# Two tiles of the second layer's attention ahead of its last query projection, and that projection's sink inside the attention pipeline

## The chip, the cores and the metric

The kernel runs as one program on one core of a Trainium2 chip. Its time is the device time of that core in microseconds (us); the times shown are medians of several runs, and the profile is of one further execution. PE is TensorE's matmul, PEld its weight load, DVE VectorE, ACT ScalarE, POOL GpSimd, SP SyncE, which issues the loads.

## The reference

A flow-matching backbone of two layers (0 and 1) with model width 1024, on 512 latent tokens and 256 context tokens. In layer 1, the last, only the latent tokens go on. Its attention half, cut to what matters:

```python
z_lat = h_lat @ w_in[l]                       # queries, keys, values, u and g in one projection
qh_l = apply_rope(rmsnorm(q_heads(q_l), q_norm_g[l]), cos, sin) * q_scale      # 8 query heads
kh_l = apply_rope(rmsnorm(kv_heads(k_l), k_norm_g[l]), cos, sin)               # 2 key heads
k_all = jnp.concatenate([kh_c, kh_l], axis=2)                                  # 256 + 512 keys
attn_lat = gqa_blocks(qh_l, k_all, v_all)                                      # softmax per query
gm_lat = chunk_gmlp(u_l, g_l, w_spatial[l], b_spatial[l], gmlp_norm_g[l])      # spatial gating
x_lat = x_lat + ga1 * (jnp.concatenate([attn_lat, gm_lat], axis=-1) @ w_out[l])
x_lat = x_lat + ga2 * sqrelu_mlp(modulate(rmsnorm(x_lat, norm2_g[l]), sh2, sc2), w_ff1[l], w_ff2[l])
```

## The kernel before

**Numbers in two parts.** Every operand of a large matmul is a pair: a high part in the fp32r format, and a low part, the rest. `split` (L226, L227) makes the pair, the high part by a cast on ACT and the low part by a subtraction on DVE or POOL. A product is three matmuls, high x high, high x low, low x high. All of them are recorded at L222, in the helper `mm`; what they do is told by their buffers.

**Layer 1 up to the attention.** The projection makes keys and values, u and g tiles, and at last the queries. `TokProj.bank` computes 256 tokens x 256 query columns into one PSUM bank (48 matmuls, in two halves of 24) and calls a sink. Four such banks give the queries: two groups (g) of four heads, two token pairs (tp) each; a head group belongs to one key head. PSUM banks of the tag b exist twice (`b0`, `b1`); `pb()` takes them in turn, or the one that `which` names. Tag a exists twice (two banks each, for scores), tag t twice (for transposes and the spatial mix).

The sink of a query bank, `sink_q`, calls `qk`: ACT squares the bank (L721), DVE sums the squares (L723), multiplies by the rotary tables (L727 and twice L731, which reads the bank last), forms the mean (L740); POOL adds the two products (L732), takes the power -1/2 (L313) and multiplies (L742). The result t1 lies in an SBUF tile of the tag w. `turned` then puts off, by the planner's count `fl.vt`, two more steps: a stack of high and low part (a cast on ACT at L747, a subtraction on DVE at L748) and its turn (8 transposes on PE at L760 and two casts on ACT at L761 into Q, `B3` to `B6`). The program calls these postponed turns the query turns; the attention forces those that it needs.

In the last query sink two things come first: the rest of the spatial mixes (`mixes`), and `make_gm`, which makes the pairs A0 to A3 of the gating output (casts L808 on ACT, subtractions L810 on DVE).

**The attention pipeline.** `pipeline` runs 32 tiles of 128 queries of one head against 768 keys, in 36 steps s. In a step stand, in this order: `scores(s)` on PE (4 matmuls into a PSUM tile pa; DVE takes the maximum, L1162), `turned_weights(s-2)` (6 transposes on PE, L1191, into two tiles pt; ACT casts them, L1193, DVE makes the low parts, L1194), `values` for the pair of tiles four steps back (6 matmuls per step, into a bank b0), `expo(s)` on ACT (L1171; its output is again a tile of the tag w, of which there are three), and one piece of filler. The filler, `out_pieces`, is the first half of the output projection, which needs the gating output alone: 32 pieces of 3 matmuls, four to a result, in bank b1; DVE adds each result to X (L1001). Steps 11, 12, 21 and 22 have no piece, step 2 has two. `mixed_heads` closes a pair of heads on DVE (L1221, L1223), and POOL writes the pair back into Q (L1225, L1226).

**What sets the order.** Up to the query banks a scheduler places the instructions on each engine by its own estimates; the whole of `pipeline` stands in `tc.manual_schedule` for PE, DVE and ACT, so there the order is that of the program text. On each engine the instructions then run in the order shown, each waiting for its own inputs and buffers.

Of the kernel before, what the change touches and what calls it, by code (L numbers as in the profile page):

```python
# [171 lines left out]
def trunk(ctx: ExitStack, tc: tile.TileContext, xT, pk1, pk2, rope, wsT, w_mod, w_tok, w_u, w_out, w_ff1, w_ff2, outT):  # L172
# [529 lines left out]
    def layer(l, h, nxt, K, kv=None, kv0=0):  # L702
# [11 lines left out]
        def qk(ps4, tp, nh, which, pool=False):  # L714
# [9 lines left out]
            t1 = te().rearrange("p (t h d) -> p t h d", t=2, h=nh) if pool and nh == 4 else tw([128, 2, nh, 64])  # L724
# [77 lines left out]
        def make_gm():  # L802
            for f in mixes:
                f()
            for g in range(4):
                gm = unit(f"A{g}", [128, 2, T])
                src = U[g // 2][:, g % 2, 0:TQ]
                act.copy(gm[:, 0, 0:TQ], src)  # L808
                with behind(maxes[3] if l == 0 and len(maxes) > 3 else None):
                    vec.tensor_tensor(out=gm[:, 1, 0:TQ], in0=src, in1=gm[:, 0, 0:TQ].bitcast(F32), op=ALU.subtract)  # L810
                GM.append(gm)

        def sink_q(grp):
            def f(tp, ps, pool=False):
                if tp == 0:
                    for f_ in mixes if grp and l else ():
                        f_()
                    Q.extend(unit(f"B{3 + grp * 2 + i}", [128, 2, T]) for i in range(2))
                ps = [p.rearrange("p (h d) -> p h d", d=64) for p in ps] if isinstance(ps, list) else ps.rearrange("p t (h d) -> p t h d", d=64)
                if last and grp and tp == NP - 1:  # L820
                    for f_ in mixes:
                        f_()
                    make_gm()
                t1 = qk(ps, tp, 4, 0, pool)
                turned(t1, 4, 0, tp, [(Q[grp * 2 + i], [(2 * i, 0), (2 * i + 1, 0)]) for i in range(2)], late(tp) + 4000.0 if pool else None)
            return f
# [163 lines left out]
        with region('q%d' % l):  # L990
            for g in range(2) if l else ():
                qp = TokProj(l, 1 + g, h, NP, sink_q(g))
                for tp in range(NP):
                    qp.bank(tp)
# [133 lines left out]

        def out_pieces():
            if not GM:  # L1130
                make_gm()
            for m in range(8):
                if m % 2 == 0:
                    wb = take("out", l, 0, m // 2)
                dst = pb(which=1)
                for k, (whi, wlo, rhi, rlo) in enumerate(w4(wb, m, GM)):
                    for i, (a, b) in enumerate(((whi, rhi), (whi, rlo), (wlo, rhi))):
                        mm(dst, a, b[:, 0:TQ], k == 0 and i == 0, k == 3 and i == 2, TQ)
                    if k < 3:
                        yield  # L1140
                gate(2, m, 0, TQ, dst)
                if m % 2:
                    release()
                yield

        def pipeline():
# [4 lines left out]
            pieces = out_pieces()  # L1151
# [45 lines left out]
            def values(g, half):  # L1197
                j, blk, hh, _ = tiles[2 * g]
                st = pairs[g // 2]
                if half == 0:  # L1200
                    st["o"] = pb(which=0)
# [15 lines left out]
            def mixed_heads(g):  # L1217
# [4 lines left out]
                if hh == 1:  # L1222
                    vec.tensor_tensor(out=mix, in0=o[:, 256:512], in1=mix, op=ALU.mult)  # L1223
                    b = slice(blk * 256, blk * 256 + 256)
                    pool_e.tensor_copy(Q[j][:, 0, b], mix)  # L1225
                    pool_e.tensor_tensor(out=Q[j][:, 1, b], in0=mix, in1=Q[j][:, 0, b].bitcast(F32), op=ALU.subtract)  # L1226
                    done[0] += 1

            for s in range(nt + 4):
                if s < nt:  # L1230
# [3 lines left out]
                    scores(s)  # L1234
                if s % 4 == 0 and 0 < s <= nt:
# [7 lines left out]
                for _ in range(0 if s in (11, 12, 21, 22) else 2 if s in (2,) else 1):  # L1243
# [4 lines left out]
            for _ in pieces:  # L1248
                fl.tick()
# [44 lines left out]
        if last:  # L1294
            fl.fillers.pop(0)
            state["slow"] = True
            with tc.manual_schedule(engines={mybir.EngineType.PE, mybir.EngineType.DVE, mybir.EngineType.Activation}):
                pipeline()
# [242 lines left out]
```

## Time and profile before

| | us |
|---|---|
| median of 3 runs (1477.64 to 1478.91) | 1478.48 |
| the profiled execution | 1480.37 |
| its span | 1478.5 |
| mean granted TensorE clock | 0.997 |

The profiled execution is 1.9 us above the median, and 1.9 us of it lie outside the span. Layer 1's last query bank and its attention stand at 981 to 1098 us of the span. A row of a timeline gives the start, the duration, the engine, the line, the operation with output and input tiles, the count, and in brackets how long the engine was idle before and what ended that. Matmuls overlap, so what one costs is read from start to start, not from its duration. The granted clock is 1.00 at full speed.

### The profile page before, as it was taken

What the parts mean: (1) busy time and instruction counts of PE and PEld (TensorE: products, weight loads), DVE (VectorE), ACT (ScalarE), POOL (GpSimd) and SP (SyncE); (2) the same over time, 40 slices, a digit from 0 to 9 for tenths busy, and PEclk for the clock granted to TensorE, in tenths of its full rate; (3) what the DMA queues carried; (4) which work ended last, traced back from release to release, by engine and by line L of the source; (5) the groups of instructions that cost most, each with busy time, mean ns of one, the idle gap of its engine ahead of it and who ended that gap; (6) DMA issues with size and microseconds to landing.
All of it is one profiled execution on the core that took longest, in us unless ns stands there. A gap on an engine that the chain in (4) does not pass through costs nothing.

```text
span 1478.5 us, 21039 instructions
## 1 busy us (share of the span) xinstructions
PE 1440.8 (97%) x8178; PEld 1227.3 (83%) x8178; DVE 911.8 (62%) x1594; ACT 638.7 (43%) x1133; POOL 369.5 (25%) x312
## 2 busy tenths in 40 slices
PE   6999999999999999999999999989999999999998
PEld 2899787988888888888888889988889888888887
DVE  5857867778766564645555547767868554444443
ACT  3552546665545443343434234537755323332221
POOL 0333512222256451323324122272222000000000
PEclk9999999999999999999999999999999999999999
DMA  9322544101233333334234212210001333223331
GB/s 368 111 72 96 191 145 143 58 1 58 95 123 126 112 134 107 129 114 134 96 124 134 76 41 75 86 58 30 30 29 63 123 100 100 94 92 100 100 100 57
DMA packets 50083, 148.71 MB, mean 101 GB/s; under 512 B 5440, under 2 KB 6976, under 8 KB 49984
## 3 DMA queue, kind: packets, MB, share of 16 engines
q1 hardware_dynamic: 49408, 146.72, 29.7%
q8 instruction: 64, 1.05, 0.3%
q10 hardware_dynamic: 576, 0.66, 0.2%
q14 instruction: 35, 0.29, 0.1%
HBM read 145.26 MB, written 2.10 MB: 100 GB/s over the span
## 4 chain that ended last, share of the span: by engine, by line
PE 86%; DVE 6%; ACT 3%; POOL 2%; issue 1%; DMA 1%; SPq 0%; POOLq 0%; ACTq 0%; DVEq 0%
PE pa L222 54%; PE pb L222 23%; PE pb L369 2%; PE pt L222 2%; PE pt L1067 2%; PE pt L1191 1%; POOL m L313 1%; ACT hi L226 1%; PE pt L760 1%; DVE lo L227 1%; DMA A<-in_w_mod 1%; POOL lo L227 1%; DVE s L922 0%; DVE X L1001 0%; DVE A L810 0%
## 5 line engine op out<-in xcount | busy, mean ns | idle before, releaser
L222 PE MATMUL pa<-A,hi 128*128 128x512 f32 (+2 forms) x1440 | 429.9, 376 | 0.6 <-DVE s L731 0.3
L226 ACT CAST hi<-raw 128x1024 fp32r<-128x1024 f32 x168 | 176.0, 1048 | 326.1 <-PE pa L222 243.3
L222 PEld LDWEIGHTS pa<-A,hi 128*128 128x128 f32 x1440 | 262.7, 188 | 46.8 <-DVE s L731 0.6
L222 PE MATMUL pa<-A,lo 128*128 128x512 f32 (+2 forms) x832 | 283.9, 347 | 0.0
L227 DVE TENSOR_TENSOR lo<-raw,hi 128x1024 fp32r<-128x1024 f32 x152 | 204.6, 1346 | 121.8 <-ACT hi L226 117.4
L418 POOL TENSOR_TENSOR C<-C,s 128x512 f32<-128x512 f32 x112 | 175.5, 1581 | 294.6 <-ACT s L417 287.8
L222 PE MATMUL pa<-B,hi 128*128 128x512 f32 x750 | 239.0, 392 | 0.0
L222 PEld LDWEIGHTS pa<-A,lo 128*128 128x128 f32 x832 | 156.7, 188 | 21.3
L1001 DVE SCALAR_TENSOR_TENSOR X<-pa,modT,X 128x512 f32<-128x512 f32 x168 | 99.7, 614 | 104.5 <-PE pa L222 103.0
L222 PEld LDWEIGHTS pa<-B,hi 128*128 128x128 f32 x750 | 139.9, 188 | 27.1
L222 PE MATMUL pb<-B,hi 128*128 128x512 f32 (+1 forms) x600 | 157.3, 350 | 2.1 <-DVE X L1001 2.0
L222 PE MATMUL pa<-B,lo 128*128 128x512 f32 (+1 forms) x450 | 155.3, 354 | 0.0
L222 PEld LDWEIGHTS pb<-B,hi 128*128 128x128 f32 x600 | 104.5, 189 | 17.5 <-DVE X L1001 3.4
L222 PE MATMUL pb<-hi,A 128*128 128x256 f32 (+1 forms) x608 | 118.1, 291 | 0.6 <-DVE m L740 0.6
L1001 DVE SCALAR_TENSOR_TENSOR X<-pb,modT,X 128x512 f32<-128x512 f32 (+3 forms) x116 | 70.7, 619 | 77.5 <-PE pb L222 77.3
L222 PE MATMUL pb<-B,lo 128*128 128x512 f32 (+1 forms) x300 | 104.0, 347 | 0.0
L222 PEld LDWEIGHTS pb<-hi,A 128*128 128x128 f32 x608 | 97.0, 191 | 2.2 <-PE pb L222 0.8
L222 PEld LDWEIGHTS pa<-B,lo 128*128 128x128 f32 x450 | 84.6, 188 | 14.8
L417 ACT ACTIVATE s<-k,silu 128x512 f32<-128x512 f32 x112 | 78.1, 718 | 37.3 <-DMA k<-in_w_mod 29.3
L222 PE MATMUL pb<-lo,A 128*128 128x256 f32 (+1 forms) x304 | 87.7, 288 | 0.0
L222 PE MATMUL pb<-A,hi 128*128 128x384 f32 (+2 forms) x288 | 82.1, 367 | 4.4 <-DVE m L740 3.4
L222 PE MATMUL pa<-B,B 128*128 128x256 f32 (+1 forms) x288 | 67.6, 350 | 0.0
(226 smaller groups left out, 2198.5 us busy)
## 6 DMA issues: line engine op xcount, KB each, us to landing
raw<-in_w_ff SPq DMA_DIRECT2D x128, 512.0 KB, 3.5
k<-in_w_mod SPq DMA_DIRECT2D x96, 256.0 KB, 2.8
raw<-in_w_tok SPq DMA_DIRECT2D x16, 512.0 KB, 3.5
raw<-in_w_out SPq DMA_DIRECT2D x16, 512.0 KB, 3.5
lo<-in_w_mod SPq DMA_DIRECT2D x16, 512.0 KB, 4.6
hi<-in_w_mod SPq DMA_DIRECT2D x16, 512.0 KB, 4.2
A<-in_w_mod SPq DMA_DIRECT2D x8, 512.0 KB, 10.0
B<-in_w_mod SPq DMA_DIRECT2D x8, 512.0 KB, 9.4
```

Of the source, the lines that this page charges most:

```text
L222: pe.matmul(out, a, b, start=start, stop=stop)
L226: act.copy(hi, src)
L227: (eng or vec).tensor_tensor(out=lo, in0=src, in1=hi.bitcast(F32), op=ALU.subtract)
L313: pool_e.tensor_tensor(out=y, in0=v, in1=mhalf[:, 0:n], op=ALU.pow)
L369: pe.matmul(ps[q:q + 32, :], S32[:, k, :], ws_[k2 // 2][:, k2 % 2 * 512:(k2 % 2 + 1) * 512], start=k < ns, stop=k >= KT - ns)
L417: act.activation(p, w, AF.Copy, scale=s)
L418: pool_e.tensor_tensor(out=a, in0=a, in1=p, op=ALU.add)
L760: pe.transpose(p[:, o:o + 128], stk[:, t, hh, c0:c0 + 128].bitcast(F32), ident)
L1001: vec.scalar_tensor_tensor(out=xs, in0=src[:, s - off:e - off], scalar=modT[l][:, i * 8 + m, cond:cond + 1], in1=xs, op0=ALU.mult, op1=ALU ...
L1067: pe.transpose(tp_[:, (kt - k0) * 128:(kt - k0) * 128 + 128], p[:, kt * 128:kt * 128 + 128], ident)
L1191: pe.transpose(tp_[:, kt * 128:kt * 128 + 128], p[:, (k0 + kt) * 128:(k0 + kt) * 128 + 128], ident)
```

## The change

The four query banks move from their own place to the place where the pipeline is called. Before the last of them (g = 1, tp = 1) come the mixes, `make_gm` and steps 0 and 1 of the pipeline; that bank is then computed and held, and its sink is called inside step 2, behind `scores(2)`. Fillers take the b bank that the last query bank does not hold, the values take the other. `make_gm` in layer 1 leaves the low parts of A2 and A3 to POOL. The t1 of layer 1's queries lie in tiles of the tag e instead of w (three of each). Steps 0 and 1 have no filler any more, nor 16 and 17, while 11, 12, 21 and 22 have one. The very last pair of heads is split on ACT and DVE, where POOL did both parts.

```diff
-            t1 = te().rearrange(...) if pool and nh == 4 else tw([128, 2, nh, 64])
+            t1 = te().rearrange(...) if (pool or l) and nh == 4 else tw([128, 2, nh, 64])
...
-                    vec.tensor_tensor(out=gm[:, 1, 0:TQ], in0=src, in1=gm[:, 0, 0:TQ].bitcast(F32), op=ALU.subtract)
+                    (pool_e if l and g > 1 else vec).tensor_tensor(out=gm[:, 1, 0:TQ], in0=src, in1=gm[:, 0, 0:TQ].bitcast(F32), op=ALU.subtract)
...
-                if last and grp and tp == NP - 1:
-                    for f_ in mixes:
-                        f_()
-                    make_gm()
...
-        with region('q%d' % l):
-            for g in range(2) if l else ():
-                qp = TokProj(l, 1 + g, h, NP, sink_q(g))
-                for tp in range(NP):
-                    qp.bank(tp)
...
-                dst = pb(which=1)
+                dst = pb(which=banks_[0])
...
-                    st["o"] = pb(which=0)
+                    st["o"] = pb(which=banks_[0] ^ 1)
...
+                    if 2 * g + 2 == nt:
+                        split(Q[j][:, 0, b], Q[j][:, 1, b], mix)
+                    else:
...
-            for s in range(nt + 4):
+            def step(s, between=None):
...
                     scores(s)
+                if between:
+                    between()
...
-                for _ in range(0 if s in (11, 12, 21, 22) else 2 if s in (2,) else 1):
+                for _ in range(0 if s < 2 or s in (16, 17) else 2 if s == 2 else 1):
                     next(pieces, None)
...
+            step, nt, rest = pipeline()
+            for g in range(2):
+                qp = TokProj(l, 1 + g, h, NP, sink_q(g))
+                for tp in range(NP):
+                    if g == 0 or tp < NP - 1:
+                        qp.bank(tp)
+                        continue
+                    for f in mixes:
+                        f()
+                    make_gm()
+                    step(0)
+                    step(1)
+                    q3 = qp.bank(tp, hold=True)
+                    banks_.append(turn_b[0])
             state["slow"] = True
             with tc.manual_schedule(engines={mybir.EngineType.PE, mybir.EngineType.DVE, mybir.EngineType.Activation}):
-                pipeline()
+                for s in range(2, nt + 4):
+                    step(s, (lambda: qp.sink(NP - 1, q3)) if s == 2 else None)
+                rest()
```

Steps 0 and 1 and the last bank now stand in the part that the scheduler places. On PE, the end of the last bank (pb_9574), the second query turn (L760, from the stack k_9587), the scores of tile 0 (pa_9678) and the first filler (pb_9688) stood thus before:

```order
L222 MATMUL pb_9574<-lo_9348,A_1408_8322 128x256
L222 MATMUL pb_9574<-hi_9347,A_1408_8322 128x256
L760 MATMUL pt_9666<-c_70,k_9587 128x128 x4
L760 MATMUL pt_9672<-c_70,k_9587 128x128 x4
L222 MATMUL pa_9678<-B_1447_8524,B_1565_9381 128x512
L222 MATMUL pa_9678<-B_1448_8525,B_1565_9381 128x512
L222 MATMUL pa_9678<-B_1447_8524,B_1565_9381 128x256
L222 MATMUL pa_9678<-B_1448_8525,B_1565_9381 128x256
L222 MATMUL pb_9688<-A_1601_9638,hi_9353 128x512 x2
L222 MATMUL pb_9688<-A_1601_9638,lo_9354 128x512
```

and on PE now, from the last scores of tile 1 (pa_9623) on; pb_9632 is the last bank, of which six matmuls and the first query turn stand ahead of tile 0, k_9598 the second stack:

```order
L222 MATMUL pa_9623<-B_1447_8524,B_1565_9381 128x256
L222 MATMUL pa_9623<-B_1448_8525,B_1565_9381 128x256
L222 MATMUL pb_9632<-hi_9128,A_1403_8317 128x256
L222 MATMUL pb_9632<-lo_9129,A_1403_8317 128x256
L222 MATMUL pb_9632<-hi_9128,A_1403_8317 128x256
L222 MATMUL pb_9632<-hi_9128,A_1404_8318 128x256
L222 MATMUL pb_9632<-lo_9129,A_1404_8318 128x256
L222 MATMUL pb_9632<-hi_9128,A_1404_8318 128x256
L222 MATMUL pb_9632<-hi_9347,A_1405_8319 128x256
L760 MATMUL pt_9601<-c_70,k_9598 128x128 x4
L760 MATMUL pt_9607<-c_70,k_9598 128x128 x4
L222 MATMUL pb_9632<-lo_9348,A_1405_8319 128x256
```

The second turn has moved from behind the bank into it: 13 of its 48 matmuls stand ahead of the turn and 35 behind it. On DVE, the gating parts (L810) and the last sink (L723 to L740) stood ahead of the first maximum (L1162):

```order
L740 TENSOR_SCALAR m_9562<-m_9562 128x8
L748 TENSOR_TENSOR k_9587<-w_9450,k_9587 128x8x64
L810 TENSOR_TENSOR A_1601_9638<-C_1469_8672,A_1601_9638 128x512
L810 TENSOR_TENSOR A_1602_9641<-C_1469_8672,A_1602_9641 128x512
L810 TENSOR_TENSOR A_1603_9644<-C_1470_8673,A_1603_9644 128x512
L810 TENSOR_TENSOR A_1604_9647<-C_1470_8673,A_1604_9647 128x512
L723 TENSOR_REDUCE m_9652<-s_9650 128x8
L727 TENSOR_TENSOR w_9654<-pb_9574,G_4439 128x512
L731 TENSOR_TENSOR s_9656<-pb_9574,G_4439 128x8x32 x2
L740 TENSOR_SCALAR m_9652<-m_9652 128x8
L1162 TENSOR_REDUCE m_9683<-pa_9678 128x1
```

and on DVE now, behind the second stack, with the maxima at L1153 and the low parts of a tile's weights at L1185:

```order
L1153 TENSOR_REDUCE m_9618<-pa_9613 128x1
L1153 TENSOR_REDUCE m_9628<-pa_9623 128x1
L810 TENSOR_TENSOR A_1597_9574<-C_1469_8672,A_1597_9574 128x512
L810 TENSOR_TENSOR A_1598_9577<-C_1469_8672,A_1598_9577 128x512
L1153 TENSOR_REDUCE m_9688<-pa_9683 128x1
L723 TENSOR_REDUCE m_9692<-s_9690 128x8
L727 TENSOR_TENSOR e_9694<-pb_9632,G_4439 128x512
L731 TENSOR_TENSOR s_9696<-pb_9632,G_4439 128x8x32 x2
L740 TENSOR_SCALAR m_9692<-m_9692 128x8
L1185 TENSOR_TENSOR A_1622_9705<-pt_9706,A_1621_9704 128x3x128
L1185 TENSOR_TENSOR A_1622_9705<-pt_9712,A_1621_9704 128x3x128
L748 TENSOR_TENSOR k_9727<-e_9564,k_9727 128x8x64
```

The sink stands behind three maxima and ahead of the first low parts, and two gating parts have left DVE. On ACT, a burst of casts for a query turn (L761), a stack (L747) and two weight blocks (L226) stood ahead of the casts of tile 3's weights (L1193):

```order
L1171 ACTIVATE w_9805,sm_9804<-pa_9770,m_9775 128x768
L747 CAST k_9810<-w_9654 128x8x64
L761 CAST B_1590_9558<-pt_9813 128x2x256
L761 CAST B_1591_9559<-pt_9819 128x2x256
L226 CAST hi_9706<-raw_9704 128x1024
L226 CAST hi_9710<-raw_9708 128x1024
L1193 CAST A_1645_9783<-pt_9836 128x3x128
```

and now, on ACT, ahead of those of tile 4 (L1184):

```order
L1162 ACTIVATE w_9831,sm_9796<-pa_9803,m_9808 128x768
L761 CAST B_1590_9558<-pt_9838 128x2x256
L761 CAST B_1591_9559<-pt_9844 128x2x256
L747 CAST k_9850<-e_9694 128x8x64
L226 CAST hi_9756<-raw_9754 128x1024
L226 CAST hi_9760<-raw_9758 128x1024
L1184 CAST A_1664_9864<-pt_9866 128x3x128
```

The burst has moved one step on. The next two weight casts on ACT move from behind the exponentials of tiles 11 and 21 to behind those of tiles 13 and 23. SP issues the same loads in the same order.

More of the change, by code (lines that the diff above doesn't have):

```diff
@@ L723, in qk @@
             vec.tensor_reduce(out=ss.rearrange("p (a b) -> p a b", b=nh), in_=sq, axis=AX.X, op=ALU.add)
-            t1 = te().rearrange("p (t h d) -> p t h d", t=2, h=nh) if pool and nh == 4 else tw([128, 2, nh, 64])
+            t1 = te().rearrange("p (t h d) -> p t h d", t=2, h=nh) if (pool or l) and nh == 4 else tw([128, 2, nh, 64])
             if tp < 2:
@@ L1127, in attention @@
                                 fl.fill0(goal)
+        banks_ = []
         def out_pieces():
-            if not GM:
-                make_gm()
             for m in range(8):
@@ L1150, in pipeline @@
             pairs, live = [{} for _ in range(nt // 4)], {}
-            pieces = out_pieces()
+            pieces, where = out_pieces(), {}
             def scores(s):
@@ L1224, in mixed_heads @@
                     b = slice(blk * 256, blk * 256 + 256)
-                    pool_e.tensor_copy(Q[j][:, 0, b], mix)
-                    pool_e.tensor_tensor(out=Q[j][:, 1, b], in0=mix, in1=Q[j][:, 0, b].bitcast(F32), op=ALU.subtract)
+                    if 2 * g + 2 == nt:
+                        split(Q[j][:, 0, b], Q[j][:, 1, b], mix)
+                    else:
+                        pool_e.tensor_copy(Q[j][:, 0, b], mix)
+                        pool_e.tensor_tensor(out=Q[j][:, 1, b], in0=mix, in1=Q[j][:, 0, b].bitcast(F32), op=ALU.subtract)
                     done[0] += 1
-            for s in range(nt + 4):
+            def step(s, between=None):
                 if s < nt:
@@ L1247, in pipeline, with rest @@
                 fl.tick()
-            for _ in pieces:
-                fl.tick()
+            def rest():
+                for _ in pieces:
+                    fl.tick()
+            return step, nt, rest
         def gm_out():
```

## The prediction

> **What bounds the kernel now.** I read the profile's page first for the engines' shares, then windows, then timelines.
>
> ```profile
> span 1478.5 us, 21039 instructions
> PE 1440.8 (97%) x8178; PEld 1227.3 (83%) x8178; DVE 911.8 (62%) x1594; ACT 638.7 (43%) x1133; POOL 369.5 (25%) x312
> ```
>
> PE is busy 97% of the span, so time can only come out of its idle 3%, out of stretches at a lower granted clock, or out of its work, which the change leaves alone. The table of five-microsecond windows (columns: length, busy time of PE, PEld, DVE, ACT and POOL with counts, granted clock, DMA share, GB/s) shows where layer 1's last query projection meets its attention:
>
> ```profile
> 990.00:995.00 5.00, 1.59 (x8) 1.23 (x7) 5.00 (x9) 0.84 (x2) 2.44 (x3) 0.92 0.00 0
> 995.00:1000.00 5.00, 5.00 (x23) 4.27 (x22) 1.02 (x2) 1.40 (x3) 3.13 (x3) 0.73 0.00 0
> 1000.00:1005.00 5.00, 3.29 (x16) 2.25 (x15) 3.88 (x6) 3.79 (x9) 0.00 (x0) 0.95 0.01 2
> 1005.00:1010.00 5.00, 5.00 (x26) 4.44 (x26) 3.13 (x7) 2.81 (x6) 0.53 (x2) 0.71 0.01 2
> ```
>
> PE is at its lowest where DVE is full, and the clock falls after each hole: the missing shares, (0.08 + 0.27 + 0.05 + 0.29) x 5 us, are 3.45 us. Then the timeline of PE (start, duration, what; in brackets the idle time before and who ended it):
>
> ```profile
> 984.25 1.04 PE L760 MATMUL pt<-c,k 128*128 128x128 f32 x8
> 985.04 0.36 PE L222 MATMUL pb<-hi,A 128*128 128x256 f32 x1
> ...
> 987.87 0.28 PE L222 MATMUL pb<-hi,A 128*128 128x256 f32 x1
> 989.07 1.09 PE L760 MATMUL pt<-c,k 128*128 128x128 f32 x8 [0.92 <-DVE k L748]
> 989.92 0.94 PE L222 MATMUL pa<-B,B 128*128 128x512 f32 x4
> 994.27 1.20 PE L222 MATMUL pb<-A,hi 128*128 128x512 f32 x2 [3.41 <-DVE m L740]
> ...
> 1003.21 1.01 PE L1191 MATMUL pt<-c,w 128*128 128x128 f32 x6 [1.60 <-DVE A L1194]
> ...
> 1021.27 0.86 PE L222 MATMUL pa<-B,B 128*128 128x512 f32 x4
> ```
>
> The last bank ends at 988.15 (987.87 + 0.28). 0.92 us go until the second query stack comes from DVE; 3.41 until the last bank's sink frees the PSUM bank for the first filler; 1.60 until DVE has the low parts of tile 0's weights. One steady step gives the price of work, by starts:
>
> ```profile
> 1024.03 0.86 PE L222 MATMUL pa<-B,B 128*128 128x512 f32 x4
> 1024.73 0.82 PE L1191 MATMUL pt<-c,w 128*128 128x128 f32 x6
> 1025.30 0.96 PE L222 MATMUL pb<-A,B 128*128 128x256 f32 x6
> 1026.10 0.63 PE L222 MATMUL pb<-A,hi 128*128 128x512 f32 x2
> ...
> 1026.79 0.86 PE L222 MATMUL pa<-B,B 128*128 128x512 f32 x4
> ```
>
> Scores 0.70, transposed weights 0.57, values 0.80, filler 0.69; a query turn is 0.79 (984.25 to 985.04). From 988.15 to tile 8's scores at 1021.27 PE did 3 turns, 8 scores, 6 weight turns, 4 values, 9 fillers: 2.4 + 5.6 + 3.4 + 3.2 + 6.2 = 20.8, and some 0.5 for changes of kind, say 21.3. So 33.1 - 21.3 = **11.8 us are lost**: 5.9 in the three waits, 3.45 in the clock, 2.4 in smaller ones.
>
> **The steps without filler** (11, 12 and 21, 22) lose too:
>
> ```profile
> 1031.77 0.95 PE L222 MATMUL pa<-B,B 128*128 128x512 f32 x4
> ...
> 1037.01 0.63 PE L222 MATMUL pb<-A,hi 128*128 128x512 f32 x2
> 1030.79 0.86 ACT L1193 CAST A<-pt 128x384 fp32r<-128x384 f32 x2 [1.01 <-PE pt L1191]
> 1033.39 1.03 ACT L226 CAST hi<-raw 128x1024 fp32r<-128x1024 f32 x1
> 1061.11 1.04 ACT L226 CAST hi<-raw 128x1024 fp32r<-128x1024 f32 x1
> ```
>
> Two bare steps are 2 x 2.07 = 4.14 of work and took 5.24, because a weight cast on ACT falls among them; the second cast, 1061.11, falls into the other pair. That is 1.1, taken for both pairs, **2.2 us**. Together 14.0 us are lost up to the last score tile; the change rearranges exactly this.
>
> **The change, part by part.** (a) The 8 score matmuls of tiles 0 and 1 now run inside the last bank, which closes the hole before them. But the second query turn moves too: it stood behind 48 bank matmuls and now stands behind 13, with 35 to follow. What it waits for does not move:
>
> ```profile
> 980.69 1.71 DVE L947 SCALAR_TENSOR_TENSOR s<-pt,gnh,k 128x256 f32<-128x256 f32 x4
> 985.99 0.76 DVE L731 TENSOR_TENSOR s<-pb,G 128x256 f32<-128x256 f32 x2 [2.05 <-POOL C L952]
> 987.16 1.85 DVE L748 TENSOR_TENSOR k<-w,k 128x512 fp32r<-128x512 f32 x1
> 992.20 0.67 DVE L723 TENSOR_REDUCE m<-s 128x8 f32<-128x512 f32 x1
> 1001.12 0.69 DVE L748 TENSOR_TENSOR k<-w,k 128x512 fp32r<-128x512 f32 x1 [2.96 <-ACT k L747]
> 1024.93 0.96 DVE L1162 TENSOR_REDUCE m<-pa 128x1 f32<-128x768 f32 x1 [0.81 <-PE pa L222]
> 1025.81 1.01 DVE L1194 TENSOR_TENSOR A<-pt,A 128x384 fp32r<-128x384 f32 x2
> 987.16 1.30 POOL L732 TENSOR_TENSOR w<-w,s 128x512 f32<-128x512 f32 x1
> 986.40 2.18 ACT L808 CAST A<-C 128x512 fp32r<-128x512 f32 x4
> 999.59 0.90 ACT L1171 ACTIVATE w<-pa,m 128x768 f32<-128x768 f32 x1 [3.44 <-PE pt L1191]
> ```
>
> DVE's and POOL's queues hold the same instructions up to that stack (the new tag only renames its input from w to e), and its chain is the wait for POOL's C in the second row, then L731, then the stack of 1.85: ready at 989.01 as before. PE gets there sooner: the spatial mix frees its first PSUM buffer at half of the 1.71, 981.55 (a wait of 0.25), then half a turn 0.4, six bank matmuls at 0.12, half a turn 0.4, two score tiles 1.4, seven matmuls 0.84: 985.3. **New wait: 3.7 us** (989.07 - 985.3), with 35 matmuls, the sink and the exponentials behind it. That PE keeps its order the trace shows: tile 0's scores use the queries of the turn at 984.25, and still started only behind the turn at 989.07.
>
> (b) The clock. The two holes of 3.41 and 1.60 us each cost a stretch at half speed, 3.45 us lost in both together, 1.7 each; the 0.92 hole cost none. A hole of 3.7 us therefore costs one such stretch, 1.7 us; bounds 0.9 (half of the stretch passes within the wait) and 2.8 (a second stretch follows such a half: 0.9 + 1.7, and 0.2 for its waits). The Trainium skill, "TensorE: Matmul & The Clock Gate", Part 1, has the half clock follow a whole idle window of about 3.4 us, free-running; by that rule a hole of 3.7 us would hardly ever drop it and the sum would be 1.7 us better. The 1.60 us hole here dropped it too, so the measurement decides.
>
> The bank then ends at 989.07 + 0.8 + 35 x 0.12 + 1.7 = 995.8. In those 6.7 us stands, on ACT, all that is queued behind the late turn: its two casts, exponentials 0 and 1 (0.90 each, and 0.2 to read the sum) and the four gating copies (2.18), 5.5 us; on DVE two maxima and two gating parts, 3.5 us. The other two gating parts are POOL's now, like L732 1.30 each, done some 2 us into the pipeline, ahead of the sink's own add and of the third filler, which asks first. So none of this is late. SP's loads keep their order.
>
> (c) The sink no longer stops the filler: it has the other bank. That removes the 3.41. The values take the bank that the sink reads, 3 us after it is done with it. But the sink's DVE work, 2.0 us (992.20 to the release at 994.27), now stands ahead of tile 0's low parts, and the PE transposes of tile 1 wait for the buffers that these free. Counted from the bank's end, PE gets there after scores, transposes, two fillers and scores, 3.4 us; DVE has the first low part after the scores (0.7), the maximum (0.9), the sink (2.0) and half of L1194 (0.5): 4.1. Wait 0.8 with the second half. The third query stack (L748) follows in DVE; in the rows it cost 0.69 alone and 1.85 where POOL's L732 began in the same moment. POOL's L732 for the sink will have begun a microsecond earlier, so it overlaps by a fifth; I take 0.9, and tile 2's transposes wait 0.65 (bounds 0.45 with 0.69, 1.7 with 1.85).
>
> The Trainium skill, "GPSIMD Engine Reference", Specifications, says that POOL shares its SBUF interfaces with VectorE, with contention for instructions of two SBUF inputs. The 0.69 and 1.85 agree; taken strictly, the stack costs 1.85 and the sum is 1.1 us worse.
>
> (d) A burst on ACT (two casts of a query turn, a stack, two weight casts of 1.03: 3.6 us) comes one step later than before, ahead of tile 4's casts, and tile 5's transposes wait for these. PE has scores, transposes, values, filler and scores to run meanwhile, 3.7 us; the burst, a cast of 0.4 and a low part of 0.5 take 4.5 for the first buffer, and the second is half a microsecond behind: 1.1 us of wait. The last query turn adds two casts to ACT in the next step: 0.25.
>
> (e) The next two weight casts now fall in steps with filler, where ACT sits idle 1.01 us in every second step (the 1030.79 row); the bare steps 16 and 17 hold none. The 2.2 us go; 0.3 stays as an estimate. If that cover were gone, 1.1 comes back at each place. With the queries' tag, exponential 1 has a buffer of its own: in the row of 999.59 it waited 3.44 us until PE had read exponential 0's, the first link to the 1.60 hole.
>
> (f) The last split goes from POOL to ACT and DVE. No wait of PE names POOL there: nothing, within 0.3 either way.
>
> **Sum.** Losses after: 0.25 + 3.7 + 1.7 + 0.8 + 0.65 + 1.1 + 0.25 + 0.3, and 0.95 for small waits (two fifths of today's 2.4, my choice: those around the blocked filler go) = 9.7. Gain 14.0 - 9.7 = 4.3 us. The profiled execution took 1480.37 (span 1478.5 and 1.9 around it), the median shown is 1478.48: 1476.1 in the first frame, **1474.2** in the second, 0.3% faster. A measurement of this kernel tells about 0.2%, 3.0 us, from no change.
>
> **The rivals.** *The clock holds* through the new hole, as it held through the one of 0.92: the 1.7 of (b) is not lost, 1472.5. Against it speaks that the 1.60 hole dropped it. The Trainium skill's rule that (b) cites would give this time too. *A second chill*: the waits of tiles 1 and 2 (0.8 + 0.65, up to 2.5 with a slow stack) lie within 4 us and together are like the 1.60 hole: another 1.7 and 1.1 of stack, 1477.0. For it: DVE is the late engine there today. *Slower: the clock never recovers.* Each stretch that holds about 1.6 us of waits is followed by another at half speed. After 3.7 come 1.5, then 1.1 us of waits, and PE at half speed is itself later. At 1.7 us each the gain is gone at (4.3 + 1.7) / 1.7 = 3.5 stretches; six give 1478.5 - 4.3 + 5 x 1.7 = 1482.7. Against it: today the clock came back after one stretch each time. *The change doesn't do what it says*, because exponentials 0 and 1 stand on ACT behind the late turn: true, but they are first asked for at 996.5, so it costs nothing.
>
> **How the numbers follow.** Forecast 0.58; clock holds 0.12; second chill 0.22; slower 0.08. Best end: 1474.2 less 1.7 (clock), 0.9 (small waits) and 0.8 (waits of (c)), 1470.8. Worst: plus 1.1 (two stretches), 1.7 and 1.0 of the second chill, 1478.0. That leaves out the slower case and some tail. Faster by over 0.2% (below 1475.5): forecast and clock holds, 0.70; within: 0.22; slower 0.08.
>
> **What would show it.** In the profile after: a wait of 3 to 4 us before the second query turn, ended by DVE's query stack, inside the last bank (a); half clock right behind it, once (b); no wait of a filler for the sink's L740 (c); waits of under 1 us at the next two weight turns, ended by L1185; no wait at the weight casts later (e). Wrong would make it: the stack at another time than 989, a clock drop after tile 2, or a hole behind the last step that takes the gain back.

## The result, and the profile after

The changed kernel takes **1471.03 us** (median of 4, 1470.36 to 1474.52) against 1478.3 of the kernel before beside it: ratio 0.9956, 95% interval 0.9938 to 0.9973. In a second series it took 1472.30 against 1478.75, ratio 0.9958 (0.9945 to 0.9970). That is 6.5 to 7.3 us faster, where 4.3 were forecast, and 0.2 us inside the best end of the range (1470.8).

The profiled execution is the slowest of the four, 1474.52. Its page, span and busy times:

```profile
span 1472.4 us, 21033 instructions
PE 1438.0 (98%) x8178; PEld 1226.7 (83%) x8178; DVE 908.4 (62%) x1593; ACT 639.5 (43%) x1134; POOL 368.7 (25%) x312
```

Its timeline of PE, the rows that answer to those of before (start, duration, line, tiles; in brackets the idle time before and what ended it):

```profile
980.10 2.79 PE L222 MATMUL pt<-ws,B 128*128 128x128 f32 x24
983.11 0.63 PE L760 MATMUL pt<-c,k 128*128 128x128 f32 x4 [0.22 <-DVE s L943]
984.64 1.64 PE L222 MATMUL pa<-B,B 128*128 128x512 f32 x8
989.26 1.97 PE L760 MATMUL pt<-c,k 128*128 128x128 f32 x8 [2.15 <-DVE k L748]
995.88 0.86 PE L222 MATMUL pa<-B,B 128*128 128x512 f32 x4
1000.18 1.01 PE L1182 MATMUL pt<-c,w 128*128 128x128 f32 x6 [0.70 <-DVE A L1185]
1002.88 1.01 PE L1182 MATMUL pt<-c,w 128*128 128x128 f32 x6 [0.30 <-DVE A L1185]
1013.19 1.01 PE L1182 MATMUL pt<-c,w 128*128 128x128 f32 x6 [0.72 <-DVE A L1185]
1083.84 0.95 PE L222 MATMUL pb<-A,B 128*128 128x256 f32 x6 [0.16 <-ACT w L1162]
1093.30 0.50 PE L222 MATMUL pb<-B,hi 128*128 128x256 f32 x2 [0.64 <-DVE X L992]
1110.35 0.51 PE L222 MATMUL pb<-B,hi 128*128 128x256 f32 x2 [0.52 <-DVE X L992]
```

The spatial mix in the first row began at 978.70 in the kernel before, so the profiled run was 1.4 late when it reached the change: it has a stretch at half clock at 180 to 185 us, where nothing was edited and the profile of before has none. Both kernels are therefore read from the mix to the end of the span: 1478.5 - 978.70 = 499.8 before, 1472.4 - 980.10 = 492.3 after, **7.5 us less**; outside the span lie 2.1 us now and 1.9 before. The tiles' scores stand inside the last bank (984.64), no filler waits for L740, and the only large wait is the predicted one, before the second query turn (989.26). Between 1013.19 and 1083.84 no row shows a wait of PE.

The window table of the same run (length, busy times with counts of PE, PEld, DVE, ACT and POOL, granted clock, DMA share, GB/s):

```profile
985.00:990.00 5.00, 2.85 (x19) 2.52 (x18) 2.95 (x7) 1.13 (x2) 4.93 (x4) 0.91 0.03 9
990.00:995.00 5.00, 5.00 (x34) 5.00 (x33) 1.72 (x4) 4.32 (x9) 2.98 (x3) 0.75 0.00 0
995.00:1000.00 5.00, 4.47 (x29) 3.84 (x27) 3.73 (x8) 3.61 (x8) 2.94 (x3) 1.00 0.01 2
```

One stretch of half clock, (0.09 + 0.25) x 5 = 1.7, stands behind the wait. And the timelines of DVE and POOL, at what ends that wait:

```profile
988.52 0.68 DVE L748 TENSOR_TENSOR k<-e,k 128x512 fp32r<-128x512 f32 x1
1000.51 0.98 DVE L748 TENSOR_TENSOR k<-e,k 128x512 fp32r<-128x512 f32 x1
...
988.54 1.80 POOL L732 TENSOR_TENSOR e<-e,s 128x512 f32<-128x512 f32 x1
```

The stack took 0.68 here, and POOL's instruction beside it 1.80; before, it was 1.85 and 1.30. The wait before the second turn ends 1.2 us sooner by that alone.

Last, behind the attention, in the rest of the output projection, PE waited three times in the kernel before until DVE had added a result to X:

```profile
1098.65 0.50 PE L222 MATMUL pb<-B,hi 128*128 128x256 f32 x2 [0.64 <-DVE X L1001]
1103.67 0.51 PE L222 MATMUL pb<-B,hi 128*128 128x256 f32 x2 [0.34 <-DVE X L1001]
1116.41 0.50 PE L222 MATMUL pb<-B,hi 128*128 128x256 f32 x2 [0.52 <-DVE X L1001]
```

From the first to the last it is 17.76 us there and 17.05 now (1093.30 to 1110.35): 0.71 us that the prediction did not have.

### The profile page after: what moved, and what is told of

Same layout as the page of the kernel before. It is cut to its first block, busy times and chain, and to the rows that moved or that the text cites. A ratio compares the mean times of both kernels' runs of the same rounds, so it can differ in the third digit from the quotient of the medians.

```text
span 1472.4 us, 21033 instructions
## 1 busy us (share of the span) xinstructions
PE 1438.0 (98%) x8178; PEld 1226.7 (83%) x8178; DVE 908.4 (62%) x1593; ACT 639.5 (43%) x1134; POOL 368.7 (25%) x312
## 4 chain that ended last, share of the span: by engine, by line
PE 86%; DVE 7%; ACT 3%; POOL 2%; issue 1%; DMA 1%; SPq 0%; POOLq 0%; ACTq 0%; DVEq 0%
PE pa L222 54%; PE pb L222 23%; PE pb L369 2%; PE pt L222 2%; PE pt L1058 2%; PE pt L1182 1%; DVE lo L227 1%; POOL m L313 1%; PE pt L760 1%; ACT hi L226 1%; DMA A<-in_w_mod 1%; DVE s L918 0%; POOL lo L227 0%; DVE X L992 0%; DVE s L731 0%
## 5 line engine op out<-in xcount | busy, mean ns | idle before, releaser
L226 ACT CAST hi<-raw 128x1024 fp32r<-128x1024 f32 x168 | 176.0, 1049 | 327.1 <-PE pa L222 242.7
L494 POOL TENSOR_TENSOR acc<-acc,s 128x256 f32<-128x256 f32 (+1 forms) x37 | 39.7, 1074 | 113.5 <-ACT s L492 113.4
```

Of the source, the lines that this page charges most:

```text
L226: act.copy(hi, src)
L494: eng.tensor_tensor(out=self.acc, in0=self.acc, in1=sq, op=ALU.add)
```

## The experiments

All twelve, with the two kernels, in one table. "Mix to end" is read from the profile as above; "clock" is what the windows from the mix to PE's last matmul lack in granted clock, times their length; "rest" is the difference. The part before the mix is the same in all of them and lost 0 to 5.1 us to half-clock stretches in these profiles. The changed kernel's own two medians differ by 1.3 us, so the rest, of one profile each, is the finer measure.

| kernel | median | ratio to before (95%) | mix to end | clock | rest |
|---|---|---|---|---|---|
| before | 1478.3 to 1479.05 | 1 | 499.8 | 3.45 | 496.4 |
| changed | 1471.03 | 0.9956 (0.9938 to 0.9973) | 492.3 | 1.7 | 490.6 |
| E1 turn behind the bank | 1472.77 | 0.9962 (0.9950 to 0.9975) | 491.6 | 0 | 491.6 |
| E2 banks swapped back | 1474.79 | 0.9976 (0.9966 to 0.9987) | 494.0 | 1.7 | 492.3 |
| E3 bare steps 11, 12 | 1473.03 | 0.9964 (0.9952 to 0.9976) | 491.3 | 0 | 491.3 |
| E4 before, banks alone | 1475.37 | 0.9981 (0.9972 to 0.9989) | 495.2 | 1.7 | 493.5 |
| E5 changed again | 1472.30 | 0.9958 (0.9945 to 0.9970) | 492.4 | 1.7 | 490.7 |
| E6 turn later in the bank | 1471.86 | 0.9950 (0.9937 to 0.9964) | 490.3 | 0 | 490.3 |
| E7 maxima first | 1471.65 | 0.9949 (0.9937 to 0.9962) | 490.6 | 0 | 490.6 |
| E8 three edits | 1473.06 | 0.9961 (0.9948 to 0.9973) | 492.4 | 1.7 | 490.7 |
| E9 stack before casts | 1472.82 | 0.9955 (0.9942 to 0.9967) | 489.4 | 0 | 489.4 |
| E10 tag back | 1475.42 | 0.9974 (0.9963 to 0.9985) | 495.3 | 1.7 | 493.6 |
| E11 gating parts on DVE | 1471.37 | 0.9945 (0.9933 to 0.9958) | 491.4 | 0 | 491.4 |
| E12 last split on POOL | 1470.95 | 0.9945 (0.9932 to 0.9958) | 490.9 | 0 | 490.9 |

E12 has the changed kernel's waits up to there and no stretch, and its rest is 490.9: a stretch costs some 1.45 to 1.7, since part of it lies in waits. Differences below 0.3 are not read.

### Which parts carry the gain

**E4, the banks alone**, in the kernel before:

```diff
-                dst = pb(which=1)
+                dst = pb(which=0)
...
-                    st["o"] = pb(which=0)
+                    st["o"] = pb(which=1)
```

> The kernel before with one edit: fillers in the PSUM bank that the last bank doesn't use, values in the other. Theory (the move is needed): the first two fillers no longer wait for L740, but tile 2's scores need the buffer that exponential 0 frees, and its maximum stands on DVE behind the sink (994.12): the 3.41 hole moves some two matmul groups on and shrinks by 2 us at most: 0 to 2 us below the kernel before, ratio 0.9986 to 1.000. Rival (the bank alone makes the gain): the 3.41 and one half-clock stretch of 1.7 go: 5.1 below, ratio 0.9965.

Its timeline of PE, and below it those of DVE and POOL:

```profile
993.82 0.97 PE L222 MATMUL pa<-B,B 128*128 128x512 f32 x4 [3.50 <-ACT w L1171]
999.39 1.01 PE L1191 MATMUL pt<-c,w 128*128 128x128 f32 x6 [0.28 <-DVE A L1194]
1093.29 0.51 PE L222 MATMUL pb<-B,hi 128*128 128x256 f32 x2 [0.63 <-DVE X L1001]
1110.35 0.50 PE L222 MATMUL pb<-B,hi 128*128 128x256 f32 x2 [0.52 <-DVE X L1001]
...
985.71 0.68 DVE L748 TENSOR_TENSOR k<-w,k 128x512 fp32r<-128x512 f32 x1
985.73 1.80 POOL L732 TENSOR_TENSOR w<-w,s 128x512 f32<-128x512 f32 x1
```

The hole is as long as before, 3.50, but it stands at tile 2's scores and is ended by exponential 0, as the theory said; the two fillers and the scores between are done by then. The rest is 2.9 less, more than the 2 allowed, but not all of it is the edit's. The second query stack took 0.68 here, where the profile of the kernel before has 1.85, though it stands ahead of anything that the banks touch; so the wait of 0.92 before the second turn is absent, and that part is no effect of the banks. Some 1.3 are the wait at the second weight turn, 0.28 in place of 1.60. The last 0.7 is a surprise: the wait of 0.34 behind the attention is gone, and the first and the last wait for X lie 17.06 apart in place of 17.76. How the banks do that, perhaps by the order in which the output projection's last groups take them, is not shown.

**E2, the banks swapped back** in the changed kernel:

```diff
-                dst = pb(which=banks_[0])
+                dst = pb(which=banks_[0] ^ 1)
...
-                    st["o"] = pb(which=banks_[0] ^ 1)
+                    st["o"] = pb(which=banks_[0])
```

> The changed kernel with the filler in the bank that the held bank uses, and the values in the other. Theory: the first filler asks at 997.15 and the sink frees the bank behind L740 at 999.57: a wait of 2.4 us ended by L740, of which the waits of 0.70 and 0.30 at the next two weight turns are absorbed: 1.4 us slower than the changed kernel, 3.1 with one more stretch of half clock. So 4.2 to 5.9 us below the kernel before (ratio 0.996 to 0.997). Rival (the bank is the whole gain): the 3.41 and its half clock come back, 5.1 us slower than the changed kernel, ratio 0.9985. Second rival (the filler has slack): no change, 0.9956.

```profile
996.38 1.06 PE L222 MATMUL pb<-A,hi 128*128 128x512 f32 x2 [2.34 <-DVE m L740]
1092.40 0.50 PE L222 MATMUL pb<-B,hi 128*128 128x256 f32 x2 [0.64 <-DVE X L992]
1097.43 0.50 PE L222 MATMUL pb<-B,hi 128*128 128x256 f32 x2 [0.34 <-DVE X L992]
1110.16 0.50 PE L222 MATMUL pb<-B,hi 128*128 128x256 f32 x2 [0.52 <-DVE X L992]
```

In this timeline of PE the filler waits 2.34 for L740, with half clock behind it, and the 0.34 behind the attention is back (1092.40 to 1110.16 is 17.76). The rest is 1.4 to 1.7 more than in the changed kernel or E12, close to the 1.4 of the theory, which left out the 0.7 behind the attention. So that 0.7 belongs to the banks, seen from both sides.

**E10, the tag back**:

```diff
-            t1 = te().rearrange(...) if (pool or l) and nh == 4 else tw([128, 2, nh, 64])
+            t1 = te().rearrange(...) if pool and nh == 4 else tw([128, 2, nh, 64])
```

> The changed kernel with the queries' first product in tag w again, whose three buffers the exponentials share. Theory (the tag is needed): two of the three are held by query products until their stacks are read, an exponential waits on ACT until PE has read an earlier one, as the 3.44 us in the kernel before, and PE then waits 1 to 3 us more between tiles 0 and 4: 491.6 to 493.6 from the mix to the end without a clock stretch (490.6). Rival (the tag costs nothing here): 490.6, no ACT wait for a transposed tile ahead of an exponential.

The timelines of ACT and of PE:

```profile
998.14 0.90 ACT L1162 ACTIVATE w<-pa,m 128x768 f32<-128x768 f32 x1 [3.38 <-PE pt L1182]
...
1002.46 1.01 PE L1182 MATMUL pt<-c,w 128*128 128x128 f32 x6 [2.30 <-DVE A L1185]
```

Exponential 2 waits 3.38 for PE to have read an earlier tile, almost the 3.44 of the kernel before, and PE's wait at the weights grows from 0.30 to 2.30. The rest is 2.7 to 3.0 more, the largest effect of one part.

**E11, the gating parts on DVE**:

```diff
-                    (pool_e if l and g > 1 else vec).tensor_tensor(out=gm[:, 1, 0:TQ], ...)
+                    vec.tensor_tensor(out=gm[:, 1, 0:TQ], ...)
```

> The changed kernel with the gating low parts 2 and 3 on DVE again instead of POOL: two more of 0.65 us there, ahead of the maximum of tile 2. Theory (DVE is idle there until PE has the scores at 996.6): the parts end at 996.9, the maximum comes 0.1 later, and the time from the mix to the end is 490.7 without a clock stretch. Rival (DVE's chain from here on sets PE's waits): all 1.3 comes back, 491.9.

```profile
997.61 1.01 PE L1182 MATMUL pt<-c,w 128*128 128x128 f32 x6 [1.17 <-DVE A L1185]
```

PE's wait at tile 1's weights is 1.17 in place of 0.70, and 0.5 to 0.8 comes back: between the two, since DVE's idle time there hides part of the 1.3.

**E12, the last split on POOL**:

```diff
-                    if 2 * g + 2 == nt:
+                    if False:
```

> The changed kernel with the last head pair's split on POOL again. Theory (the changed kernel's 0.7 us behind the last step, a wait of 0.34 and 0.37 of other time that are gone, come from this split): 491.3 from the mix to the end without a clock stretch, and the wait of 0.34 for X before the third group of the second half of the output projection is back. Rival (as predicted, nothing within 0.3): 490.6, no such wait; the 0.7 then come from the filler's places.

The first two waits for X lie 17.05 apart without the 0.34 between them, as in the changed kernel: the split costs nothing and gains nothing.

**E3, bare steps 11 and 12** in place of 16 and 17:

```diff
-                for _ in range(0 if s < 2 or s in (16, 17) else 2 if s == 2 else 1):
+                for _ in range(0 if s < 2 or s in (11, 12) else 2 if s == 2 else 1):
```

> The changed kernel with the bare steps 11 and 12 in place of 16 and 17. Theory: the weight cast of about 1.03 us on ACT falls among bare steps again, and the pair takes 1.1 us more than its work: 1.1 us slower than the changed kernel, 6.2 below the kernel before (ratio 0.9958 to 0.9966), with a wait of PE of about 1 us in steps 11 to 13. Rival (what makes the loss is not the cast but the late query turn that the bare steps 16 and 17 cover): then the pair 16 and 17 loses as well, and the time is 2 us or more above the changed kernel. Second rival: nothing.

Its timeline of PE at the bare steps, and of ACT at the next weight cast:

```profile
1021.82 0.86 PE L222 MATMUL pa<-B,B 128*128 128x512 f32 x4
1024.03 0.95 PE L222 MATMUL pa<-B,B 128*128 128x512 f32 x4
1026.58 0.86 PE L222 MATMUL pa<-B,B 128*128 128x512 f32 x4
...
1030.19 1.04 ACT L226 CAST hi<-raw 128x1024 fp32r<-128x1024 f32 x1
```

The run did not test what it was to test: two fillers fewer have run by then than in the kernel before, so the cast falls behind the bare pair. The pair still takes 4.76, 0.62 over its 4.14 of work (in the changed kernel, at 16 and 17, it takes 4.14). In the kernel before, the scores of steps 11 to 13 start at 1029.56, 1031.77 and 1034.32: the bare pair took the same 4.76 there, and step 13 lost another 0.62 up to its filler at 1037.01. Here step 13 takes 2.77 with its filler and loses nothing. So 0.62 comes from the place alone; the cast stands beside the other 0.62 in the kernel before, and that it made it fits but is not shown. The rival doesn't hold: steps 16 and 17, with filler here, show no wait of PE.

### What the wait before the second turn costs

**E5, the changed kernel again**:

> The changed kernel once more, unedited, beside the others of this series. Its runs so far lie from 1470.36 to 1474.52, and its profile holds three half-clock stretches (0 to 25, 150 to 200, 985 to 995 us). Theory (which stretches fall is chance, the waits are not): from the spatial mix to the end again 490.6 us, plus 1.7 if the stretch behind the second query turn falls and nothing if it doesn't; the wait before that turn again 2.1 to 2.2, L748 again 0.68. Rival (the wait drops the clock each time): 492.3. Median between 1470.4 and 1473, ratio 0.995 to 0.9965.

Wait 2.17, L748 0.68, rest 490.7, and the stretch fell again. But of the seven profiles with that wait (changed, E2, E3, E5, E10, E11, E12: 2.12 to 2.17) only the changed kernel's and this one have half clock behind it. E3's windows, for one:

```profile
985.00:990.00 5.00, 2.87 (x26) 2.66 (x25) 3.54 (x6) 1.81 (x4) 5.00 (x4) 1.00 0.00 0
990.00:995.00 5.00, 5.00 (x40) 4.78 (x39) 2.52 (x4) 4.75 (x12) 3.57 (x4) 1.00 0.00 2
```

What tells them apart can be read. In windows of 0.25 us a stretch of half clock lasts 3.41 or 3.42 us (twice that at 185 us in E7 and E8), and within one run the stretches begin a whole number of such lengths apart: in the changed kernel at 19.73, 180.16 and 989.12 us, 47 and then 237 times 3.413; in the kernel before at 21.45, 994.25 and 1004.49, 285 and 3 times. So each run can be laid out in cells of 3.413 us, and a wait falls into one cell or across two:

| run | wait | idle time of PE in the two cells | half clock behind |
|---|---|---|---|
| changed | 2.15 | 2.02 and 0.14 | yes |
| E5 | 2.17 | 2.17 and 0 | yes |
| E2 | 2.14 | 1.03 and 1.12 | no |
| E3 | 2.13 | 1.57 and 0.56 | no |
| E10 | 2.13 | 1.40 and 0.73 | no |
| E11 | 2.12 | 0.77 and 1.35 | no |
| E12 | 2.13 | 0.46 and 1.67 | no |

From the mix to 1025 us, in all 14 profiles, each of the seven cells with 1.98 us or more of idle time is followed by a stretch, and none with 1.40 or less is; of the five between (1.57 to 1.87) one is, with 1.71 in the kernel before. Idle time is not the whole measure: before the mix, at 182 us, a cell with 0.99 idle was followed by a stretch in E7. So what is chance is where the cells lie in a run.

**E1, the turn behind the bank**:

```diff
-                    if s % 8 == 0:
-                        for f in turns[0:3 + NP * (1 + s // 16)]:
+                    if s % 4 == 0:
+                        for f in turns[0:3 + NP * (1 + s // 16) - (s == 0)]:
```

> The changed kernel with one edit: the second query turn isn't asked for before tile 0 but by step 4, and stands behind the last bank. Theory (the hole is one of order): PE never waits inside the bank, so the 2.15 us before that turn and the 1.7 us of half clock behind it go; the turn's two ACT casts now stand ahead of tile 0's first cast, at most 0.5. So 3.3 us below the changed kernel, some 10.6 below the kernel before (ratio 0.993), and no wait of PE between the mix and the end of the bank beyond 0.3. Rival (the hole moves): PE gets to the first transposed weights 3.85 us sooner, and what it waits for there (exponential 0, the gating parts, all on ACT and DVE) is as late as now: a wait of 2 to 4 us behind the bank, and the time of the changed kernel, ratio 0.9956.

Its timelines of PE, ACT and DVE:

```profile
992.57 1.03 PE L1182 MATMUL pt<-c,w 128*128 128x128 f32 x6 [2.22 <-ACT B L761]
1009.85 1.01 PE L1182 MATMUL pt<-c,w 128*128 128x128 f32 x6 [2.64 <-DVE A L1185]
...
991.93 1.07 ACT L761 CAST B<-pt 128x512 fp32r<-128x512 f32 x2
...
1006.94 1.52 DVE L748 TENSOR_TENSOR k<-e,k 128x512 fp32r<-128x512 f32 x1 [3.96 <-ACT k L747]
```

The theory of order falls, the rival holds: 2.22 stand behind the bank, because the turn's casts now queue on ACT behind exponential 0, the gating copies and exponential 1. A second wait, 2.64, comes with tile 5: with the turn, a later stack was asked for after the weight casts.

**E6, the turn 11 matmuls later in the bank** (E1's edit, and the turn asked for inside the bank):

```diff
+                    fl.defer(2000.0, turns[4])
                     q3 = qp.bank(tp, hold=True)
```

> The changed kernel with the second query turn 11 bank matmuls later on PE (behind 24 of the 48 instead of 13). ACT then takes exponentials 0 and 1 ahead of the turn's first cast, and the four gating copies ahead of its second. Theory (ACT and DVE bound this stretch, PE's order only moves the wait): PE comes to the turn 1.3 us later, 0.85 of the 2.15 stays; the second cast is done at about 995.6 in the time of the changed kernel's profile, and the first transposed weights, asked for at 993.6, wait for its buffer: 1.5 to 2. From the mix to the end 490 to 491, that is within 0.7 of the changed kernel. Rival (the wait was one of PE's order): 0.85 stays and nothing comes behind: 1.3 less, 489.3, with 1.7 less again where the clock holds.

```profile
989.13 1.09 PE L760 MATMUL pt<-c,k 128*128 128x128 f32 x8 [0.84 <-DVE k L748]
994.95 0.55 PE L1182 MATMUL pt<-c,w 128*128 128x128 f32 x3 [0.82 <-ACT B L761]
```

0.84 as worked out, and 0.82 behind it (1.5 to 2 expected): the rest is 490.3, nearly unmoved.

**E7, the maxima first on DVE**: the second last bank is held too, and its sink follows step 1, with L731 ordered behind the maximum of tile 1.

```diff
+                    with tc.issue_after(hold_[0].ins) if hold_ else nullcontext():
                       vec.tensor_tensor(out=t2[:, :, :, o], ...)
...
                     step(1)
+                    hold_.append(mx_[1])
+                    qp.sink(0, q2)
+                    hold_.clear()
```

> The changed kernel with the sink of the second but last query bank behind the maximum of tile 1: DVE takes maximum 0, then the stack L748, then maximum 1, then L731, which waits for POOL's C. So L748 starts at 986.8 (in the time of the changed kernel's profile), while POOL's L948 runs (986.07 to 988.58). Theory (a two-input DVE instruction that starts second waits for POOL's): L748 takes 1.8 to 2.2, the second turn, behind 15 bank matmuls now, still waits 1.4 to 1.6; exponential 0 runs 3 us sooner: from the mix to the end 489.5 to 490.2 without a clock stretch. Rival (the stack is late only because it stands behind L731): L748 takes 0.69, the turn waits 0 to 0.3, and 488 to 488.7 remain.

DVE, POOL and PE (lines moved by one or two: L749 is the stack, L950 the second mix product):

```profile
986.15 1.12 DVE L749 TENSOR_TENSOR k<-e,k 128x512 fp32r<-128x512 f32 x1 [0.22 <-ACT k L748]
...
985.42 2.98 POOL L950 TENSOR_TENSOR C<-s,C 128x512 f32<-128x512 f32 x2
...
987.42 1.06 PE L761 MATMUL pt<-c,k 128*128 128x128 f32 x8 [0.70 <-DVE k L749]
996.98 1.01 PE L1184 MATMUL pt<-c,w 128*128 128x128 f32 x6 [1.11 <-DVE A L1187]
```

Neither number was met: the stack took 1.12, POOL's two instructions 2.98 in place of 2.51, the first 1.30 and the second 1.72. The stack began while the first ran (985.42 and 1.30 is 986.72) and ended 0.55 behind it, at 987.27: the reading is that it waited for the first and held up the second. The wait fell to 0.70 and came back at tile 1's weights; the rest is unmoved.

**E8, three edits** (E7's, the turn inside the bank, and the last sink behind the first transposed weights):

```diff
-                if between:
-                    between()
...
                     turned_weights(s - 2)
+                if between:
+                    between()
```

> Three edits of the changed kernel: maxima 0 and 1 ahead of L731 on DVE as above; the second query turn behind 24 of the last bank's matmuls; the last sink behind the first transposed weights. Theory (DVE's and ACT's chain bounds the stretch, so the edits add up only as far as they shorten it): before the turn at most 0.5 of wait, no wait at tile 1's weights, about 1.3 at tile 2's: 1.7 in place of 3.15, from the mix to the end 489.2 without a clock stretch (490.6 in the changed kernel), 1.4 us faster than it. Rival (all of the 3.15 goes): 487.5. Rival (the waits only move): 490.6.

**E9, the stack's cast sooner**, on top of E8:

```diff
-            fl.defer(PAR["QK%d" % l] if wait is None else wait, one)
+            fl.defer(PAR["QK%d" % l] - (500.0 if len(turns) == 7 else 0.0) if wait is None else wait, one)
```

> The three edits of the run before, and a fourth: the cast of the second last query stack (ACT) is asked for 0.5 us sooner by the planner's clock, so that it stands ahead of the two weight casts and not behind them. Theory (the 2.35 us before tile 5's transposes came from that order: the cast behind 2.01 of weight casts, the stack beside POOL's L227, the maximum of tile 7 behind the stack): 0.7 of the 2.35 stays, as in the changed kernel: from the mix to the end 489.1 without a clock stretch (490.7 before this edit), 1.5 below the changed kernel. Rival (the stretch has a bound of its own, whatever the order): 490.6 again, with the wait somewhere else.

E8's timelines of PE, ACT and DVE, then E9's of PE and ACT:

```profile
1014.35 1.01 PE L1184 MATMUL pt<-c,w 128*128 128x128 f32 x6 [2.35 <-DVE A L1187]
...
1008.88 2.01 ACT L226 CAST hi<-raw 128x1024 fp32r<-128x1024 f32 x2
1010.78 0.62 ACT L748 CAST k<-e 128x512 fp32r<-128x512 f32 x1
...
1011.43 1.53 DVE L749 TENSOR_TENSOR k<-e,k 128x512 fp32r<-128x512 f32 x1 [4.11 <-ACT k L748]
```

```profile
1009.53 1.03 PE L1184 MATMUL pt<-c,w 128*128 128x128 f32 x6 [0.58 <-ACT B L762]
...
1008.37 0.62 ACT L748 CAST k<-e 128x512 fp32r<-128x512 f32 x1 [0.89 <-PE pt L761]
1009.86 2.01 ACT L226 CAST hi<-raw 128x1024 fp32r<-128x1024 f32 x2
```

E8 removed the wait before the turn altogether, and 2.35 appeared at tile 5, as in E1; its rest is that of the changed kernel, so its rival held. E9 moved one cast ahead of two and the 2.35 went: rest 489.4 (489.1 expected), 1.2 to 1.5 less than the changed kernel. Its median, 1472.82, doesn't show that; its profile has 3.4 us of half clock before the mix. It is not shown to be faster.

PE's bracketed waits of 0.2 or more from the mix to 1016 us sum to 4.1 in the changed kernel, 5.1 in E1, 3.3 in E6 and E7, 3.9 in E8 and 2.2 in E9. The rest less that sum is 486.5, 486.5, 487.0, 487.2, 486.8 and 487.2: the waits explain it within 0.8, and what counts is their sum over the stretch, not the one that was removed.

## Why the prediction was right, and where not

The direction held and the range held narrowly; the gain was 2.2 to 3.0 us larger than forecast. Term by term, in the profiled run:

| term | forecast loss | measured |
|---|---|---|
| (a) first turn | 0.25 | 0.22 |
| (a) second turn | **3.7** | **2.15** |
| (b) half clock | 1.7 | 1.7 in this run, in 2 profiles of 7 |
| (c) tiles 1 and 2 | 0.8 + 0.65 | 0.70 + 0.30 |
| (d) tile 5, last turn | 1.1 + 0.25 | 0.72 + 0 |
| (e) later casts | 0.3 | 0 |
| (f) last split | 0, within 0.3 | 0 (E12) |
| waits for X behind the attention | not seen | 0.7 gained (E2, E4) |

**The mis-sized term is (a), 1.55 us.** It took the stack's 1.85 over "as before", though its rows show another L748 at 0.69. PE came 0.4 later than worked out (989.26 - 2.15 - 1.4 = 985.7, not 985.3), and the stack was done 1.2 sooner (989.26 - 1.4 = 987.9, not 989.07), because it began 0.02 us ahead of POOL's L732 and not with it. In all nine profiles in which DVE keeps that order in the changed kernel (changed, E1 to E3, E5, E6, E10 to E12) it began 0.01 to 0.02 ahead and took 0.68; in the kernel before both begin at 987.16, and it took 1.85. The 1.85 is not even the kernel before's own: E4, which has its queues up to there, shows 0.68 (985.71, POOL 985.73) and no wait before its second turn. So 1.85 stands in one profile of eleven, and the prediction priced the stack, and today's 0.92, from that one execution. Why the starts differ is open: up to there the queues hold the same instructions.

The Trainium skill, "SBUF — State Buffer", section "SBUF: two separate sides", has a DVE instruction with two SBUF inputs and a POOL instruction that reads SBUF take a shared pair of SBUF ports as a lock for a whole instruction, which goes to the one that starts first. The pairs here agree: 1.85 and 1.30 where both began at 987.16 (before), as if POOL was served first; DVE first, 0.68 and 1.80; DVE between two of POOL's, 1.12 (E7). A price for that stack needed the order of two starts.

**(b) hung on (a).** A wait of 3.7 us, wherever it falls, puts at least 1.85 us of idle time into one cell of 3.413, near the 1.98 from which every cell dropped the clock: an estimate from the cells above by which (b) was nearly certain at that length. At 2.15 it was a chance, and that the profiled run shows it is luck. The rival "the clock holds" had 0.12; it is what five of seven profiles show. From the mix on, waits of 3.41 and 3.50 (before, E4) dropped the clock, of thirteen between 1.6 and 2.65 six did, and none below 1.2 did. Counted at 6/13, the term is 0.8. The Trainium skill's rule that (b) weighed, "TensorE: Matmul & The Clock Gate", Part 1, would let none of the thirteen drop it; the measurement decides against that, while the free-running window of about 3.4 us in the same rule agrees with the cells.

**(c), (d) and (e)** were 1.4 too high together; (c) and (d) had the right places and releasers (L1185 each time), and (e) the right outcome. The 5.24 of (e) is not that of the two bare steps: it runs from step 12's scores to step 13's filler, and the pair 11 and 12 took 4.76 in the kernel before (see under E3). The small waits were too low: from the mix to the first wait for X it is 1098.65 - 978.70 = 119.95 before and 1093.30 - 980.10 = 113.2 now, so 14.0 - 6.75 = 7.25 are still lost, and the rows above make 5.8 of it; 1.45 are left where 0.95 was put. The sum comes out: 4.3 + 1.55 + 1.4 - 0.5 + 0.7 = 7.5. The second chill and the slower case did not come.

**The bank change was right for its reason and incomplete**: it removes the filler's wait (E2 brings 2.34 back), but by itself only moves the hole to tile 2's scores (E4), and it also takes 0.7 out of the waits for X far behind.

That the exponentials need buffers which no query product holds had no price of its own; E10 shows 2.7 to 3.0 us, the largest of the parts that were put back. Against the changed kernel and E12 (490.6 and 490.9) the parts bring back 1.4 to 1.7 (banks), 2.7 to 3.0 (tag), 0.5 to 0.8 (gating parts), 0.4 to 0.7 (bare steps) and nothing (split): 5.0 to 6.2, where the rest fell by 5.5 to 5.8. Some 0.9 of that fall is the slow stack of the one profile of before (E4), so the agreement is loose, and parts put back one at a time need not add up. Moving the tiles without these parts was not run, so what the move is worth alone stays open.

## What to carry to other kernels

Where several engines' queues are nearly full over a stretch of 30 us, sum the waits of that stretch: removing the largest one, by a turn that is asked for later (E1) or a maximum that comes first (E7), gave back what it took until the last link, one cast in front of two others, was reordered as well (E9, by its rest; its median doesn't show it). A buffer's tag or bank can be worth more than the move for which it was changed, and it can change waits far behind. And price two instructions that hold each other up by which starts first, with both ends in the sum, and from more than one execution.

## What the runs showed of the hardware

A wait of about 2 us of PE drops the clock to half in some executions and not in others: with the wait of 2.12 to 2.17 us two profiles of seven show it, those in which it falls almost whole into one cell of 3.413 us. Where the cells lie differs from run to run. Up to the mix, where all kernels are the same, the profiles lost 0, 1.7, 3.4 or 5.1 us to such stretches. Single runs of one kernel differ by as much, and their mean granted clock goes with it at the ends (in E1 1471.30 at 1.000 and 1476.54 at 0.995); that the stretches make all of the difference is not shown.

Of two instructions of DVE and POOL that begin within 0.02 us of each other, either can be the one held up: the stack and POOL's add took 0.68 and about 1.80 us in ten profiles, 1.85 and 1.30 in one.
